# Two transformer blocks on one Trainium2 core: the expert layer's dense planes in two arithmetics, its stream buffers and its vector work rearranged

## The chip, the core and the metric

The kernel runs on one core of one Trainium2 chip. A core has five engines that follow their own instruction lists in order and wait for each other by semaphores: TensorE (PE in the profile; its weight loads have a row of their own, PEld), VectorE (DVE), ScalarE (ACT), GpSimd (POOL) and SyncE (SP), which here only starts transfers. Data are in SBUF (128 partitions); products accumulate in PSUM banks of 512 fp32 columns. The metric is the device time of one execution in microseconds (us), lower is better.

## The reference, cut to what matters

Two blocks follow each other on a sequence of 256 tokens of width 1024. The first has two kinds of attention and then the expert layer, the second has convolution, attention, retention, attention to a memory and a squared-relu MLP. The change is in the expert layer and in the few instructions on either side of it:

```python
def peer_ffn(x, w_query, sub_keys, expert_down, expert_up):
    ...
        q = (xc @ w_query).reshape(C, PEER_HEADS, 2, PEER_HALF)
        sc = jnp.einsum('thpd,hpnd->thpn', q, sub_keys).astype(jnp.float32)
        top_s, top_i = lax.top_k(sc, PEER_TOPK)
        ...
        best_s, best_pos = lax.top_k(cand_s, PEER_TOPK)
        experts = jnp.take_along_axis(cand_i, best_pos, axis=-1)
        gates = jax.nn.softmax(best_s, axis=-1)
        u = expert_down[experts]
        vv = expert_up[experts]
        act = jax.nn.gelu(jnp.einsum('cd,chkd->chk', xc, u).astype(jnp.float32), approximate=False)
        w = (gates * act).astype(xc.dtype)
        return jnp.einsum('chk,chkd->cd', w, vv)
```

There are 8 heads, 128 sub-keys on each of two sides, so 16384 experts, of which each token takes 16 per head: 128 experts per token.

## The kernel before, in words

The expert layer does not gather all its experts. For the last ND = 192 tokens it computes every expert: the 16384 rows of each table are cut into 128 planes of 128 experts, and a plane (512 KB, a tile of 128 x 1024 fp32) goes through TensorE whole. Only for the first NS = 64 tokens are rows gathered, by indirect transfers on POOL, 128 rows of 1024 numbers at a time.

**Queries.** `norm_d` makes the normed input in two parts, `xh` + `xl` (tiles `fh`, `fl`; type float32r, the sum is the fp32 value). 16 chunks of `peer_query` come by `stream`: SP loads `raw`, ACT rounds it to `hi` (line 61), DVE takes `lo` = raw - hi (line 62), and `gemm_t` makes three products per 128 rows: hi with xh, hi with xl, lo with xh (lines 98 to 100). `xf` (tile `ff`) = xh + xl for the 192 tokens is added on POOL. `rows` = the normed input of the first 64 tokens, scaled by a gain row that comes by DMA (line 647).

**Lists.** For each half t of the tokens DVE picks the top 16 scores and the best 16 pairs per head (lines 665 to 729). The result, `lists`, is transposed by TensorE (line 732) into `i1T`, `i2T`, `powT`, `gT`. The two halves share scratch, and a scheduler mixes their instructions on DVE.

**The first stage** runs over the 128 planes of the down table, two at a time. `stream_whole` loads a plane into any of nine buffers (three each of the tags raw, hi, lo), and `whole_plane` multiplies it in fp32 with `xf`, 8 products of 192 columns per plane (line 817); in the trace each of them is two MATMUL records and two LDWEIGHTS records. Into these planes three other things are woven: `gates_of` (from plane J0 = 34 on) builds one-hot tables for TG = 4 tokens on DVE and ACT (lines 797 to 802) and TensorE multiplies them into a gate table (line 806) that is written over, or multiplied into, `slots`; ACT applies gelu to each pair of planes; and `step` handles one gathered row per call: 64 times `dot` (line 751: fetched row times `rows`, summed), then 64 times `axpy` (line 761: fetched row times a scalar, added to `sums`). KD = 92 of the 128 steps are spread over the planes from plane 24 on, the other 36 over the first 112 planes of the second stage. `fetched` has five buffers.

**The second stage** runs over the 128 planes of the up table. Each comes by `stream` (three `raw`, three `hi`, three `lo` buffers); ACT and DVE make `a2` from `slots` (lines 879 to 881), and `ups` does ten products of 512 columns per plane (lines 865 to 870). The last LASTN = 3 planes are held back so that the sums of the two halves end one after the other. For the first 64 tokens the sum sits in other partitions than the residual: ACT copies it (`moved`, line 894), DVE adds twice. Norm and transposes of the next stage follow.

The order of instructions on each engine is set by the tile scheduler from the program; `tc.keep_in_program_order` pins an instruction to its place. `tc.high_priority` lets `split` go ahead of other work.

Of the kernel before, what the change touches and what calls it, by code (L numbers as in the profile page):

```python
# [40 lines left out]
def layers_kernel(ctx: ExitStack, tc: tile.TileContext, a: dict, out: bass.AP, upto: str = "all"):  # L41
# [28 lines left out]

    def stream(src):
        if ahead:
            return ahead.pop(0)
        raw = stream_p.tile([P, CH], F32, name="raw", tag="raw", bufs=3)
        nc.sync.dma_start(raw, src)
        own = more["at"] % (3 + more["n"]) < 3
        more["at"] += 1
        pool, b = (stream_p, 3) if own else (more["pool"], more["n"])
        hi = pool.tile([P, CH], F32R, name="hi", tag="hi", bufs=b)
        lo = pool.tile([P, CH], F32R, name="lo", tag="lo", bufs=b)  # L80
        with tc.high_priority():
            split(raw, hi, lo)
        return hi, lo
# [486 lines left out]
    with ExitStack() as c2:  # L570
# [3 lines left out]
        xl = fx.tile([P, KT, T], F32R, name="fl")  # L574
        xf = pr.tile([P, KT, ND], F32, name="ff")
        slots = pr.tile([P, P, ND], F32, name="slots")
        TG = 4
        NG = T // TG
# [24 lines left out]
        rs_peer = norm_d(x_sb, ss_peer, 1, xh, xl, prs)  # L603
        G.tensor_tensor(xf, f32v(xh[:, :, NS:]), f32v(xl[:, :, NS:]), op=OP.add)


        def fetched():
            return pr.tile([P, D], F32, name="fetched", tag="fetched", bufs=5)

# [14 lines left out]

        ranks = carve([P, 2, 16, P], BF)
        for hq in range(4):
            pss = [at_tile() for _ in range(NT)]
            for q in range(4):
                hp = hq * 4 + q
                o = mm_tile()  # L630
                gemm_t(o[:, :T], xh, xl, stream(a["peer_query"][hp]))
                qT = prs.tile([P, T], F32, name="qT", tag="oh1")
                S.copy(qT, o[:, :T])
                if hq > 0 and q < 3:
                    c = (hq - 1) * 3 + q
                    if c < 8:
                        rs, cs = ranks[:, c // 4, c % 4 * 4:c % 4 * 4 + 4], iota16b[:, c // 4, c % 4 * 4:c % 4 * 4 + 4, None]
                        tc.keep_in_program_order(S.copy(rs, cs.to_broadcast([P, 4, P])))
# [5 lines left out]
        grow = fetched()  # L644
        nc.scalar.dma_start(grow, bass.AP(tensor=a["ffn_gain"].tensor, offset=0, ap=[[0, P], [1, D]]))
        rows = pr.tile([P, D], F32, name="rows_s", tag="rows_s")
        V.scalar_tensor_tensor(rows[:NS], x_sb[:NS, 0, :], rs_peer[0][:NS], grow[:NS], op0=OP.mult, op1=OP.mult)
        S.copy(rows[NS:], rows[:NS])
        tc.keep_in_program_order(V.tensor_copy(iota, iota_f[:, :, None].to_broadcast([P, P, 2])))
# [5 lines left out]
        powT = pr.tile([P, T], BF, name="powT")  # L655
        gT = [pr.tile([P, T], dt, name="gT%d" % i) for i, dt in enumerate((F16, F32))]
        floor = top[0]
        for t in range(NT):
# [37 lines left out]
            for i in range(2):  # L696
                V.copy_predicated(keyu[:, i, :], keyu[:, 4, :], keyu[:, 2 + i, :])
            lists = carve([P, 5, P])
            oh = carve([P, 16, P], BF)
# [29 lines left out]
            V.tensor_tensor(scaled, scaled, inverse, op=OP.mult)  # L729
            tp = tp_tile()  # L730
            for i in range(4):
                PE.transpose(tp[:, i * P:(i + 1) * P], lists[:, i, :], ident)
            ts = slice(t * P, (t + 1) * P)
            S.copy(i1T[:, ts], tp[:, 0:P])
            S.copy(i2T[:, ts], tp[:, P:2 * P])
            S.copy(powT[:, ts], tp[:, 3 * P:4 * P])
            S.copy(gT[0][:, ts], tp[:, 2 * P:3 * P])
            V.tensor_tensor(gT[1][:, ts], tp[:, 2 * P:3 * P], gT[0][:, ts], op=OP.subtract)

# [13 lines left out]

        sums = pr.tile([P, D], F32, name="sums")

# [28 lines left out]
        def gates_of(g, j):  # L784
# [3 lines left out]

            shape = [P, TG // 2, P, 2]
            oh1, oh2 = (prs.tile(shape, dt, name=n, tag=n) for n, dt in (("oh1", BF), ("oh2", F16)))  # L790
            og = [prs.tile(shape, F16, name="og%d" % i, tag="og%d" % i) for i in range(2)]
            places = iota[:, None, :, :].to_broadcast(shape)
# [8 lines left out]
            for k in range(TG):  # L801
                S.mul(og[1][:, k // 2, :, k % 2], oh2[:, k // 2, :, k % 2], gT[1][:, g * TG + k:g * TG + k + 1])
            ps = at_tile()
            for k in range(TG):
                for i in range(2):
                    PE.matmul(ps[:, k * P:(k + 1) * P], oh1[:, k // 2, :, k % 2], og[i][:, k // 2, :, k % 2],
                              start=(i == 0), stop=(i == 1))
            gv = ps.rearrange("p (t j) -> p j t", t=TG)
            sv = slots[:, :, cs]
            if j > 0:  # L810
                V.tensor_tensor(sv[:, :j], gv[:, :j], sv[:, :j], op=OP.mult)
            if j < P:
                S.copy(sv[:, j:], gv[:, j:])

# [6 lines left out]
        K0 = 12  # L821
        KD = 92
        for jp in range(P // 2):
# [5 lines left out]
            while state["k"] < KD * (jp - K0 + 1) // (P // 2 - K0):  # L829
                step()  # L830
            nt = state["g"] * TG - NS
            o = mm_tile()
            for jj in range(2):
                whole_plane(o[:, jj * ND:(jj + 1) * ND], stream_whole(a["peer_down"][j + jj]))
            ov = o[:, :2 * ND].rearrange("p (j t) -> p j t", j=2)
# [37 lines left out]
        for j in range(P):  # L873
            while state["k"] < min(2 * HALF, KD + -(-(2 * HALF - KD) * (j + 1) // KU)):
                step()
            uh, ul = stream(a["peer_up"][j])

            a2 = prs.tile([P, 7 * NS], F32R, name="a2", tag="oh1")
            S.copy(a2[:, :ND], slots[:, j, :])  # L879
            S.copy(a2[:, ND:T], slots[:, j, :NS])  # L880
            V.tensor_tensor(a2[:, T:], slots[:, j, :], f32v(a2[:, :ND]), op=OP.subtract)
            if j >= P - LASTN:
                held.append((j, (uh, ul, a2)))
            else:
                for t in range(NT):
                    ups(j, (uh, ul, a2), t)
        moved = fetched()
# [472 lines left out]
```

## Time and profile before

| what | value |
|---|---|
| median of 3 runs | 1474.74 us (1473.08 to 1474.85) |
| the profiled execution | 1476.18 us, of which the span from the first to the last instruction is 1474.4 us |
| mean granted TensorE clock | 0.996 |
| TensorE busy | 1429.4 us, 97% of the span |
| VectorE, ScalarE, GpSimd busy | 982.8 us, 716.4 us, 265.5 us |
| moved from and to memory | 336.90 MB, 228 GB/s over the span |

A busy share is a mean over stages that have different limits. The expert layer takes about half of the span: queries from about 158 us, the first stage from 226 to 589 us, the second from 589 to 923 us. A TensorE record is drawn until its results are out, so that records overlap: the distance from one start to the next tells what an instruction costs in a full stream, not its drawn length.

### The profile page before, as it was taken

How to read it: one execution, taken by the hardware profiler on the slowest of the kernel's cores; microseconds unless marked ns; L12 is line 12 of the kernel's file. 1: busy time of each engine (PE TensorE's matmuls, PEld its weight loads, DVE VectorE, ACT ScalarE, POOL GpSimd, SP SyncE). 2: the span in 40 equal slices, each digit the busy share in tenths (PEclk: the TensorE clock that was granted, in tenths of full speed). 3: DMA queues.
4: the chain of work that ended last, by engine and by line, in shares of the span. 5: the costliest groups of instructions: out<-in, count | busy, mean ns of one | idle time of the engine just before them, and what ended most of it. 6: DMA issues, size and time to landing. Idle time of an engine off the chain costs nothing. (4 is left out here: it accounts for less than half of the span.)

```text
span 1474.4 us, 23648 instructions
## 1 busy us (share of the span) xinstructions
PE 1429.4 (97%) x8728; PEld 1265.8 (86%) x8728; DVE 982.8 (67%) x1884; ACT 716.4 (49%) x1448; POOL 265.5 (18%) x223
## 2 busy tenths in 40 slices
PE   9999899999999999989999999899999999999998
PEld 7778799999999999667676778797899989899886
DVE  7975568957767776767766776554475555566653
ACT  6565552224333332555555565574444455565442
POOL 4621100134343323211111100031101100000000
PEclk9999999999999999999999999999999999999999
DMA  7434558599999998878878767544356554366553
GB/s 271 153 125 158 177 188 298 193 382 349 341 351 337 351 347 301 295 251 267 263 252 274 260 213 228 198 156 140 118 169 192 186 186 155 125 205 192 192 186 115
DMA packets 93700, 336.90 MB, mean 228 GB/s; under 512 B 10736, under 2 KB 12656, under 8 KB 92816
## 3 DMA queue, kind: packets, MB, share of 16 engines
q1 hardware_dynamic: 73376, 259.79, 52.7%
q0 software_dynamic: 19344, 73.41, 14.0%
q10 hardware_dynamic: 864, 2.19, 0.4%
q8 instruction: 69, 1.13, 0.3%
q14 instruction: 47, 0.39, 0.1%
HBM read 331.15 MB, written 4.19 MB: 227 GB/s over the span
## 5 line engine op out<-in xcount | busy, mean ns | idle before, releaser
L62 DVE TENSOR_TENSOR lo<-raw,hi 128x1024 fp32r<-128x1024 f32 x356 | 439.4, 1235 | 303.6 <-ACT hi L61 302.5
L61 ACT CAST hi<-raw 128x1024 fp32r<-128x1024 f32 x356 | 373.3, 1049 | 413.8 <-PE mm L99 112.9
L817 PE MATMUL mm<-ff,whole 128*128 128x192 f32 x2048 | 345.3, 328 | 0.0
L817 PEld LDWEIGHTS mm<-ff,whole 128*128 128x128 f32 x2048 | 333.2, 191 | 0.0
L98 PE MATMUL mm<-rows_h,hi 128*128 128x256 f32 x736 | 204.0, 283 | 2.1 <-ACT qT_x L1198 1.1
L100 PE MATMUL mm<-rows_h,lo 128*128 128x256 f32 x736 | 204.6, 280 | 1.0 <-DVE lo L62 1.0
L99 PE MATMUL mm<-rows_l,hi 128*128 128x256 f32 x736 | 204.8, 280 | 0.0
L98 PEld LDWEIGHTS mm<-rows_h,hi 128*128 128x128 f32 x736 | 137.4, 189 | 3.6 <-ACT hi L61 1.4
L100 PEld LDWEIGHTS mm<-rows_h,lo 128*128 128x128 f32 x736 | 138.5, 189 | 1.6 <-DVE lo L62 1.6
L99 PEld LDWEIGHTS mm<-rows_l,hi 128*128 128x128 f32 x736 | 138.6, 189 | 0.6
L745 POOL DMA_INDIRECT fetched<-in_peer_up,picks x64 | 77.3, 1208 | 274.7 <-DVE sums L761 255.0
L838 ACT ACTIVATE slots<-mm 128x384 f32<-128x384 f32 (+43 forms) x60 | 22.4, 373 | 200.2 <-PE mm L817 200.1
L868 PE MATMUL mm<-hi,a 128*128 128x512 f32 x256 | 103.3, 403 | 16.6 <-ACT a L879 16.5
L745 POOL DMA_INDIRECT fetched<-in_down_rows,picks x64 | 81.5, 1273 | 176.9 <-DVE fetched L751 105.1
L865 PE MATMUL mm<-hi,a 128*128 128x512 f32 x256 | 104.2, 407 | 3.4 <-ACT a L879 2.4
L866 PE MATMUL mm<-lo,a 128*128 128x512 f32 x256 | 101.5, 396 | 0.0
L869 PE MATMUL mm<-lo,a 128*128 128x512 f32 x256 | 101.3, 396 | 0.0
L870 PE MATMUL mm<-hi,a 128*128 128x512 f32 x256 | 81.1, 397 | 0.0
L761 DVE SCALAR_TENSOR_TENSOR sums<-fetched,acts,sums 128x1024 f32<-128x1024 f32 x63 | 80.5, 1277 | 0.1
L751 DVE SCALAR_TENSOR_TENSOR fetched<-fetched,rows_s 128x1024 f32<-128x1024 f32 x64 | 75.8, 1216 | 6.3 <-DMA fetched<-in_down_rows,picks 6.3
L868 PEld LDWEIGHTS mm<-hi,a 128*128 128x128 f32 x256 | 48.1, 188 | 35.6 <-ACT a L879 24.7
L865 PEld LDWEIGHTS mm<-hi,a 128*128 128x128 f32 x256 | 48.2, 188 | 27.9 <-ACT a L879 8.1
(376 smaller groups left out, 2506.6 us busy)
## 6 DMA issues: line engine op xcount, KB each, us to landing
whole<-in_peer_down SPq DMA_DIRECT2D x128, 512.0 KB, 5.7
raw<-in_peer_up SPq DMA_DIRECT2D x128, 512.0 KB, 4.6
raw<-in_w_in_2t SPq DMA_DIRECT2D x52, 512.0 KB, 3.5
raw<-in_w_up SPq DMA_DIRECT2D x32, 512.0 KB, 4.3
raw<-in_w_down SPq DMA_DIRECT2D x32, 512.0 KB, 4.3
raw<-in_w_in SPq DMA_DIRECT2D x24, 512.0 KB, 3.9
raw<-in_peer_query SPq DMA_DIRECT2D x16, 512.0 KB, 4.1
raw<-in_w_in_2n SPq DMA_DIRECT2D x12, 512.0 KB, 3.4
```

What stands on the lines that cost most here:

```text
L61: S.copy(hi, src)
L62: V.tensor_tensor(lo, src, f32v(hi), op=OP.subtract)
L98: PE.matmul(o, hi, xh[:, k, :], start=(k == 0), stop=False)
L99: PE.matmul(o, hi, xl[:, k, :], start=False, stop=False)
L100: PE.matmul(o, lo, xh[:, k, :], start=False, stop=(k == kts - 1))
L745: G.indirect_dma_start(out=r, out_offset=None, in_=tables[table], in_offset=bass.IndirectOffsetOnAxis(ap=picks[:, k:k + 1], axis=0))
L817: PE.matmul(o, w[:, k * P:(k + 1) * P], xf[:, k, :], start=(k == 0), stop=(k == KT - 1))
L865: PE.matmul(acc[0][hf], both, uh[:, ds], start=first, stop=False)
L866: PE.matmul(acc[0][hf], both, ul[:, ds], start=False, stop=last)
L868: PE.matmul(acc[1][hf], high, uh[:, ds], start=first, stop=False)
L869: PE.matmul(acc[1][hf], high, ul[:, ds], start=False, stop=False)
L870: PE.matmul(acc[1][hf], low, uh[:, ds], start=False, stop=last)
```

## The change

Eight edits in the expert layer, and what follows from the first for the order on POOL:

1. In the first stage, from plane JS = 24 on, every odd plane goes through `stream` and `gemm_t` instead of `stream_whole` and `whole_plane`: 24 products of 192 columns in float32r (hi with xh, hi with xl, lo with xh) in place of 8 in fp32. That is 52 planes.
2. KD falls from 92 to 76: 16 steps move to the second stage, which then has 52.
3. In the second stage `raw` gets six chunks: the three buffers of before for planes 0 to 2 of every six, then `raw_o` (in the memory of the one-hot tables, two buffers) for planes 3 and 5 and `raw_f` (in the memory of `xf`) for plane 4. The two ACT copies into `a2` are pinned to program order and written ahead of `stream`.
4. One-hot tables are built for TG = 8 tokens per call, in 128 x 1024 instructions; the products of a call go to two PSUM tiles of four tokens.
5. The transposes of `lists` are written at planes 14 and 28 (`turn`) and pinned; each half has a `lists` table of its own.
6. `xf` is added on DVE, and it and `rows` are written between the query groups.
7. `fetched` has four buffers, and `sums` shares memory with `rows`.
8. The sums for the first 64 tokens are added straight from PSUM; the ACT copies `moved` go.
9. Since split planes read `fh` and `fl` until the end of the first stage, the two loads of the memory's normed rows into that place (`nh`, `nl`, 1 MB each, on POOL), which are issued at the start of the first stage in the kernel before, stand after the 16th gather of up rows in POOL's list, that is at the end of the first stage.

```diff
-    def stream(src):
+    def stream(src, raw=None):
         if ahead:
             return ahead.pop(0)
-        raw = stream_p.tile([P, CH], F32, name="raw", tag="raw", bufs=3)
+        if raw is None:
+            raw = stream_p.tile([P, CH], F32, name="raw", tag="raw", bufs=3)
         nc.sync.dma_start(raw, src)
...
-        TG = 4
+        TG = 8
...
-        G.tensor_tensor(xf, f32v(xh[:, :, NS:]), f32v(xl[:, :, NS:]), op=OP.add)
...
-            return pr.tile([P, D], F32, name="fetched", tag="fetched", bufs=5)
+            return pr.tile([P, D], F32, name="fetched", tag="fetched", bufs=4)
...
+        def unsplit():
+            tc.keep_in_program_order(V.tensor_tensor(xf, f32v(xh[:, :, NS:]), f32v(xl[:, :, NS:]), op=OP.add))
+
+        def scaled_rows():
+            tc.keep_in_program_order(V.scalar_tensor_tensor(rows[:NS], x_sb[:NS, 0, :], rs_peer[0][:NS], grow[:NS],
+                                                            op0=OP.mult, op1=OP.mult))
+            tc.keep_in_program_order(S.copy(rows[NS:], rows[:NS]))
+
         for hq in range(4):
+            if hq in (1, 2):
+                (unsplit if hq == 1 else scaled_rows)()
...
-        V.scalar_tensor_tensor(rows[:NS], x_sb[:NS, 0, :], rs_peer[0][:NS], grow[:NS], op0=OP.mult, op1=OP.mult)
-        S.copy(rows[NS:], rows[:NS])
...
-            tp = tp_tile()
-            for i in range(4):
-                PE.transpose(tp[:, i * P:(i + 1) * P], lists[:, i, :], ident)
...
+            def turn(t=t, lists=lists):
+                tp = tp_tile()
+                for i in range(4):
+                    tc.keep_in_program_order(PE.transpose(tp[:, i * P:(i + 1) * P], lists[:, i, :], ident))
...
-        sums = pr.tile([P, D], F32, name="sums")
+        sums = pr.tile([P, D], F32, name="sums", tag="rows_s")
...
-        KD = 92
+        KD = 76
+        JS = 24
...
+            if j in (14, 28):
+                turns[j // 14 - 1]()
...
             for jj in range(2):
-                whole_plane(o[:, jj * ND:(jj + 1) * ND], stream_whole(a["peer_down"][j + jj]))
+                ot, src = o[:, jj * ND:(jj + 1) * ND], a["peer_down"][j + jj]
+                if j >= JS and jj == 1:
+                    gemm_t(ot, xh[:, :, NS:], xl[:, :, NS:], stream(src))
+                else:
+                    whole_plane(ot, stream_whole(src))
...
-            uh, ul = stream(a["peer_up"][j])
 
             a2 = prs.tile([P, 7 * NS], F32R, name="a2", tag="oh1")
-            S.copy(a2[:, :ND], slots[:, j, :])
-            S.copy(a2[:, ND:T], slots[:, j, :NS])
+            tc.keep_in_program_order(S.copy(a2[:, :ND], slots[:, j, :]))
+            tc.keep_in_program_order(S.copy(a2[:, ND:T], slots[:, j, :NS]))
+            raw = None
+            if j % 6 > 2:
+
+                raw = pr.tile([P, KT * ND], F32, name="raw_f", tag="ff")[:, :CH] if j % 6 == 4 else                     prs.tile([P, CH], F32, name="raw_o", tag="ohs")
+            uh, ul = stream(a["peer_up"][j], raw)
...
                 if t == 0:
-                    S.copy(moved[NS:, ds], acc[0][hf][:NS])
-                    V.tensor_tensor(x_sb[NS:, 0, ds], acc[0][hf][NS:], x_sb[NS:, 0, ds], op=OP.add)
-                    V.tensor_tensor(x_sb[NS:, 0, ds], moved[NS:, ds], x_sb[NS:, 0, ds], op=OP.add)
+                    for part in (acc[0][hf][NS:], acc[0][hf][:NS]):
+                        tc.keep_in_program_order(V.tensor_tensor(x_sb[NS:, 0, ds], part, x_sb[NS:, 0, ds], op=OP.add))
```

DVE's list while the queries are computed, first before, then with the change (`fl` are the low parts of the normed input, eight in all):

```order
L198 SCALAR_TENSOR_TENSOR fl<-tp,gcols,fh 128x256 x5
L647 SCALAR_TENSOR_TENSOR rows_s<-x_sb,rrow,fetched 64x1024
L649 CAST iota<-slots 128x256
L198 SCALAR_TENSOR_TENSOR fl<-tp,gcols,fh 128x256 x3
L62 TENSOR_TENSOR lo<-raw,hi 128x1024 x5
```

```order
L199 SCALAR_TENSOR_TENSOR fl<-tp,gcols,fh 128x256 x8
L62 TENSOR_TENSOR lo<-raw,hi 128x1024
L631 TENSOR_TENSOR ff<-fh,fl 128x1536
L62 TENSOR_TENSOR lo<-raw,hi 128x1024 x4
L634 SCALAR_TENSOR_TENSOR rows_s<-x_sb,rrow,fetched 64x1024
```

The scaled rows moved behind all eight `fl` and five `lo`, and the sum for `xf` came onto DVE.

DVE's list where the second half's lists are finished (the last `slots<-slots 128x16x8` of a half, line 709 before and 720 now, is what TensorE's transposes of it wait for), first before, then with the change:

```order
L798 TENSOR_TENSOR oh_3257<-iota,i2T 128x512
L706 TENSOR_TENSOR slots<-slots 128x2048
L725 TENSOR_SCALAR slots<-slots 128x128
L708 TENSOR_TENSOR slots<-slots 128x1024
L726 TENSOR_SCALAR slots<-slots 128x128
L708 TENSOR_TENSOR slots<-slots 128x512
L728 TENSOR_SCALAR slots<-slots 128x128
L708 TENSOR_TENSOR slots<-slots 128x256
L729 TENSOR_TENSOR slots<-slots 128x128
L709 TENSOR_TENSOR slots<-slots 128x16x8
L738 TENSOR_TENSOR gT_2393<-tp,gT_2392 128x128
L751 SCALAR_TENSOR_TENSOR fetched,acts<-fetched,rows_s 128x1024 x8
```

```order
L766 SCALAR_TENSOR_TENSOR fetched,acts<-fetched,rows_s 128x1024 x3
L720 TENSOR_TENSOR slots<-slots 128x16x8
L62 TENSOR_TENSOR lo<-raw,hi 128x1024
L766 SCALAR_TENSOR_TENSOR fetched,acts<-fetched,rows_s 128x1024
L714 TENSOR_TENSOR slots<-slots 128x2048
L717 TENSOR_TENSOR slots<-slots 128x2048
L62 TENSOR_TENSOR lo<-raw,hi 128x1024
L766 SCALAR_TENSOR_TENSOR fetched,acts<-fetched,rows_s 128x1024 x2
L719 TENSOR_TENSOR slots<-slots 128x1024
L719 TENSOR_TENSOR slots<-slots 128x512
L719 TENSOR_TENSOR slots<-slots 128x256
L720 TENSOR_TENSOR slots<-slots 128x16x8
```

Six dots and two `lo` now stand ahead of the end of the lists in this piece, and one more dot and two more `lo` shortly above it; before, the first dot came after that end. On TensorE the first transpose of the first half stands at the same place in both kernels (after three products of plane 18). The last three of the second half stood after two products of plane 26 and now stand after ten products of plane 31.

## Rows read from the trace of the kernel before

**Rows 1.** Engines by stretch: busy us with count, clock, DMA share, GB/s

```profile
226.00:320.00 94.00, 91.77 (x561) 91.35 (x560) 77.68 (x382) 20.93 (x46) 16.98 (x15) 0.98 0.78 278
320.00:560.00 240.00, 240.00 (x1702) 237.22 (x1701) 177.94 (x400) 92.52 (x314) 88.60 (x74) 1.00 0.96 349
589.00:840.00 251.00, 231.97 (x945) 173.83 (x945) 176.12 (x220) 135.63 (x282) 44.46 (x33) 0.99 0.81 266
840.00:923.00 83.00, 82.06 (x348) 64.06 (x347) 58.12 (x74) 49.74 (x102) 0.00 (x0) 1.00 0.71 226
923.00:940.00 17.00, 13.02 (x59) 10.32 (x58) 13.73 (x21) 10.87 (x21) 3.22 (x4) 0.91 0.69 234
```

**Rows 2.** Timeline of TensorE, second stage: start, length, line, what

```profile
655.08 0.40 PE L868 MATMUL mm<-hi,a 128*128 128x512 f32 x1
...
657.41 0.40 PE L868 MATMUL mm<-hi,a 128*128 128x512 f32 x1
```

**Rows 3.** Waits in the second stage: us in total, times, longest

```profile
ACT hi L61 <- DMA raw<-in_peer_up: 61.3, 30, 3.7
...
PE mm L868 <- ACT a L879: 16.5, 14, 1.9
```

**Rows 4.** Timeline of ScalarE, second stage; idle time before it in brackets

```profile
660.38 1.04 ACT L61 CAST hi<-raw 128x1024 fp32r<-128x1024 f32 x1 [3.66 <-DMA raw<-in_peer_up]
```

**Rows 5.** Transfers of the up planes: count, KB each, median us to landing

```profile
raw<-in_peer_up SPq DMA_DIRECT2D x128, 512.0 KB, 4.6
```

**Rows 6.** Costliest groups of the page, VectorE: busy us, mean ns

```profile
L62 DVE TENSOR_TENSOR lo<-raw,hi 128x1024 fp32r<-128x1024 f32 x356 | 439.4, 1235 | 303.6 <-ACT hi L61 302.5
...
L761 DVE SCALAR_TENSOR_TENSOR sums<-fetched,acts,sums 128x1024 f32<-128x1024 f32 x63 | 80.5, 1277 | 0.1
```

**Rows 7.** Timeline of DVE, ACT and PE, queries

```profile
175.32 1.28 DVE L647 SCALAR_TENSOR_TENSOR rows_s<-x_sb,rrow,fetched 64x1024 f32<-64x1024 f32 x1 [4.91 <-DMA fetched<-in_ffn_gain]
...
177.25 0.39 PE L99 MATMUL mm<-fl,hi 128*128 128x256 f32 x1 [2.80 <-DVE fl L198]
```

**Rows 8.** Timeline of TensorE, first stage, fp32 planes between the transposes

```profile
276.68 0.33 PE L732 MATMUL tp<-ident,slots 128*128 128x128 f32 x1 [2.23 <-DVE slots L709]
276.84 9.97 PE L817 MATMUL mm<-ff,whole 128*128 128x192 f32 x50
...
299.44 0.49 PE L732 MATMUL tp<-ident,slots 128*128 128x128 f32 x3
299.77 20.32 PE L817 MATMUL mm<-ff,whole 128*128 128x192 f32 x124
```

**Rows 9.** DVE by line, first stage (320 to 560 us): busy us, mean ns

```profile
L751 DVE SCALAR_TENSOR_TENSOR fetched<-fetched,rows_s 128x1024 f32<-128x1024 f32 x56 | 66.3, 1216 | 0.0
...
L797 DVE TENSOR_TENSOR oh<-iota,i1T 128x512 bf16<-128x512 bf16 x46 | 19.2, 418 | 0.0
```

**Rows 10.** Timeline of TensorE, queries, 256 columns; 27 products from first to last

```profile
222.44 0.28 PE L98 MATMUL mm<-fh,hi 128*128 128x256 f32 x1
...
225.50 0.28 PE L100 MATMUL mm<-fh,lo 128*128 128x256 f32 x1
```

**Rows 11.** Timeline of TensorE, first block: fp32 products of 64 columns

```profile
131.42 1.89 PE L506 MATMUL mm<-vm,pT 128*128 128x64 f32 x16
133.15 1.04 PE L164 MATMUL tp<-ident,ho 128*128 128x128 f32 x8
```

**Rows 12.** Weight loads by shape, whole program: busy us, mean ns

```profile
L98 PEld LDWEIGHTS mm<-rows_h,hi 128*128 128x128 f32 x736 | 137.4, 189 | 3.6 <-ACT hi L61 1.4 <-ACT qT_x L1198 1.3 <-ACT rows_h L197 0.4
...
L806 PEld LDWEIGHTS <-oh 128*128 128x128 bf16 x384 | 25.8, 97 | 3.0
...
L506 PEld LDWEIGHTS mm<-vm,pT 128*128 128x128 f32 x48 | 5.9, 191 | 0.0
```

**Rows 13.** Timeline of TensorE behind the second stage

```profile
933.59 0.41 PE L190 MATMUL tp<-ident,xs 128*128 128x128 f32 x2 [1.68 <-issue]
936.30 1.12 PE L190 MATMUL tp<-ident,xs 128*128 128x128 f32 x6 [2.31 <-DVE xs L208]
```

More of the change, by code (lines that the diff above doesn't have):

```diff
@@ L574, in layers_kernel @@
         xl = fx.tile([P, KT, T], F32R, name="fl")
-        xf = pr.tile([P, KT, ND], F32, name="ff")
+        xf = pr.tile([P, KT, ND], F32, name="ff", tag="ff")
         slots = pr.tile([P, P, ND], F32, name="slots")
-        TG = 4
+        TG = 8
         NG = T // TG
@@ L625, in layers_kernel @@
         ranks = carve([P, 2, 16, P], BF)
+        grow = fetched()
+        nc.scalar.dma_start(grow, bass.AP(tensor=a["ffn_gain"].tensor, offset=0, ap=[[0, P], [1, D]]))
+        rows = pr.tile([P, D], F32, name="rows_s", tag="rows_s")
+        def unsplit():
[4 more added lines that the diff above has]
+            tc.keep_in_program_order(S.copy(rows[NS:], rows[:NS]))
         for hq in range(4):
+            if hq in (1, 2):
+                (unsplit if hq == 1 else scaled_rows)()
             pss = [at_tile() for _ in range(NT)]
@@ L642, in layers_kernel @@
                 S.copy(sc[t][:, hq * 4:hq * 4 + 4, :].rearrange("p a b -> p (a b)"), pss[t])
-        grow = fetched()
-        nc.scalar.dma_start(grow, bass.AP(tensor=a["ffn_gain"].tensor, offset=0, ap=[[0, P], [1, D]]))
-        rows = pr.tile([P, D], F32, name="rows_s", tag="rows_s")
-        V.scalar_tensor_tensor(rows[:NS], x_sb[:NS, 0, :], rs_peer[0][:NS], grow[:NS], op0=OP.mult, op1=OP.mult)
-        S.copy(rows[NS:], rows[:NS])
         tc.keep_in_program_order(V.tensor_copy(iota, iota_f[:, :, None].to_broadcast([P, P, 2])))
@@ L656, in layers_kernel @@
         gT = [pr.tile([P, T], dt, name="gT%d" % i) for i, dt in enumerate((F16, F32))]
+        turns = {}
+        tables_of = [carve([P, 5, P]) for _ in range(NT)]
         floor = top[0]
@@ L697, in layers_kernel @@
                 V.copy_predicated(keyu[:, i, :], keyu[:, 4, :], keyu[:, 2 + i, :])
-            lists = carve([P, 5, P])
+            lists = tables_of[t]
             oh = carve([P, 16, P], BF)
@@ L729, in layers_kernel @@
             V.tensor_tensor(scaled, scaled, inverse, op=OP.mult)
-            tp = tp_tile()
-            for i in range(4):
-                PE.transpose(tp[:, i * P:(i + 1) * P], lists[:, i, :], ident)
[L733 to L738, printed above, removed]
+            def turn(t=t, lists=lists):
+                tp = tp_tile()
+                for i in range(4):
+                    tc.keep_in_program_order(PE.transpose(tp[:, i * P:(i + 1) * P], lists[:, i, :], ident))
+                ts = slice(t * P, (t + 1) * P)
+                S.copy(i1T[:, ts], tp[:, 0:P])
+                S.copy(i2T[:, ts], tp[:, P:2 * P])
+                S.copy(powT[:, ts], tp[:, 3 * P:4 * P])
+                S.copy(gT[0][:, ts], tp[:, 2 * P:3 * P])
+                V.tensor_tensor(gT[1][:, ts], tp[:, 2 * P:3 * P], gT[0][:, ts], op=OP.subtract)
+            turns[t] = turn
         tables = {n: a[n].rearrange("a b d -> (a b) d") for n in ("down_rows", "peer_up")}
@@ L789, in gates_of @@
             shape = [P, TG // 2, P, 2]
-            oh1, oh2 = (prs.tile(shape, dt, name=n, tag=n) for n, dt in (("oh1", BF), ("oh2", F16)))
-            og = [prs.tile(shape, F16, name="og%d" % i, tag="og%d" % i) for i in range(2)]
+            oh1 = prs.tile(shape, BF, name="oh1", tag="oh1")
+            ohs = prs.tile([P, 2, TG // 2, P, 2], F16, name="ohs", tag="ohs")
+            oh2 = ohs[:, 0]
+            og = [ohs[:, 1], prs.tile(shape, F16, name="og1", tag="og1")]
             places = iota[:, None, :, :].to_broadcast(shape)
@@ L802, in gates_of @@
                 S.mul(og[1][:, k // 2, :, k % 2], oh2[:, k // 2, :, k % 2], gT[1][:, g * TG + k:g * TG + k + 1])
[L803 to L813, printed above, removed]
+            for part in range(0, TG, 4):
+                ps = at_tile()
+                for k in range(part, part + 4):
+                    c = (k - part) * P
+                    for i in range(2):
+                        PE.matmul(ps[:, c:c + P], oh1[:, k // 2, :, k % 2], og[i][:, k // 2, :, k % 2],
+                                  start=(i == 0), stop=(i == 1))
+                gv = ps.rearrange("p (t j) -> p j t", t=4)
+                sv = slots[:, :, cs.start + part:cs.start + part + 4]
+                if j > 0:
+                    V.tensor_tensor(sv[:, :j], gv[:, :j], sv[:, :j], op=OP.mult)
+                if j < P:
+                    S.copy(sv[:, j:], gv[:, j:])
         def whole_plane(o, w):
@@ L886, in layers_kernel @@
                     ups(j, (uh, ul, a2), t)
-        moved = fetched()
         for t in range(NT):
```

## The prediction

> **What bounds the kernel now.** I read the engines by stretch first [rows 1]. TensorE is drawn busy for all of 320 to 560 us, and for 232.0 of 251 us in the second stage as long as rows are gathered there. Where no row is gathered (840 to 923 us) it is busy for 82.1 of 83 us. So TensorE sets the pace of the first stage, and the second loses time beside the gathers.
>
> How much is lost is read from the distance of products. In the second stage the tenth product after the one at 655.08 us starts at 657.41 us: 0.233 us each, 2.33 us per plane [rows 2]. The 945 products of 589 to 840 us [rows 1] would need 220.2 us and took 251: 30.8 us lost. The 348 behind them would need 81.1 us and took 83: 1.9 us. Together 32.7 us over what TensorE needs.
>
> The waits say why [rows 3]. TensorE waits for ACT's `a2` (16.5 us in 14 waits; the rest hides in overlapping records). ACT's list has the rounding of the next plane ahead of this `a2`, and that rounding waits for the plane's transfer: 61.3 us in 30 waits, as at 660.38 us [rows 4]. Three `raw` chunks explain it: a chunk's place turns over every 3 x 2.33 = 7.0 us, of which rounding (1.04) [rows 4] and difference (1.24) [rows 6] take 2.3. That leaves 4.7 us for a transfer whose median landing is 4.6 us [rows 5]. Any delay by a gather is a stall.
>
> **Six raw chunks, the largest term.** A place then turns over every 14.0 us, and 14.0 - 2.3 = 11.7 us are left for a landing. The longest wait seen was 3.7 us [rows 3], so 7 us more cover every one. Two things can eat into this. The rate: 128 planes and 52 gathers, 52/112 of a chunk beside each of the first 112 planes, are 1.464 x 0.524 MB per 2.33 us = 329 GB/s; the first stage moves 349 GB/s while TensorE is busy throughout [rows 1], so it fits, closely. And `nh`, `nl`, 2.1 MB, now start with the second stage: 6 us of that rate. VectorE has room: 176.1 us busy over 94.5 planes [rows 1] is 1.86 us per plane, 16 more axpys of 1.277 us [rows 6] over 112 planes make it 2.04 of 2.33. The pinned `a2` copies change nothing by themselves: in ACT's list the next plane's rounding still precedes them. I let 5 of the 32.7 us stand: **-27.7 us** (bounds -33 and 0).
>
> **The scaled rows moved.** In the queries DVE stands at line 647 for 4.91 us for the gain row, three `fl` are queued behind it, and TensorE waits 2.80 us for one of them [rows 7]. Now all `fl` precede it: **-2.8 us**. The sum for `xf`, 128 x 1536, comes onto DVE behind them; the nearest row, 1.24 us for 128 x 1024 [rows 6], makes some 1.9 us of it. DVE has idle time there, and TensorE meets the queries' next `lo` with several chunks in hand, so I cost it at nothing; uncovered it is 1.9 us.
>
> **The transposes of the lists.** The first half's first transpose stays in plane 18, and DVE's work ahead of it stays too, so its stall of 2.23 us, and the 10 us after it in which 50 products take 9.97 us instead of 8.2 (the granted clock of this stretch is 0.98 [rows 1], part of it on the 1.2 GHz level), remain [rows 8]. The second half's change. Before, no wait is shown at 299.44 us, 22.8 us behind the first transpose [rows 8]. Now seven dots (1.216 us each [rows 9]) and four `lo` (1.235) are ahead on DVE, 13.4 us, and eight one-hot instructions of double length instead of ten short ones: between 8 and 16 times 0.418 us [rows 9], so up to 2.5 us more. The lists end 36 to 39 us behind the first transpose, later still if a dot waits for its gather. TensorE gets there after 13 planes of 2.6 us plus the 1.8 us of low clock: 36 us. A tie, at a place where a stall also costs clock: **+4 us** (bounds 0 and 9).
>
> **The split planes.** A whole plane is 16 records, 124 of which take 20.32 us: at most 0.164 us each, 2.62 us per plane [rows 8]. A split plane is 24 records of 192 columns in float32r, a shape that the trace does not have. Two rows bound it from below. Float32r products of 256 columns start 3.06/26 = 0.1177 us apart [rows 10], those of 512 columns 0.233 [rows 2]: 0.45 ns per column, which gives 0.0889 us for 192. But a product also loads 128 x 128 weights, and where columns are few the load shows: fp32 products of 64 columns start 1.73/16 = 0.108 us apart [rows 11]. The load record of float32r weights is as long as fp32's (189 against 191 ns; bf16 97) [rows 12]. So I take 0.108 us, the row that is like it in its load: 24 x 0.108 = 2.59 us, 0.03 less than whole. Over 52 planes **-1.6 us**. Bounds: 0.0889 gives -25; the 256-column distance gives 2.82 us per plane, +11; at the top, a product that costs what the fp32 product of 192 columns costs (two records, 0.328 us) gives +273.
>
> [...]
>
> VectorE must carry 52 `lo` more in the 294 us of planes 24 to 127: 64 us, less 16 dots, 19.5 us; one-hots between no change and 40 us less. From 177.9 of 240 us [rows 1], 218 of 294, it comes to 222 to 262 us, 89% at most. ACT takes 52 roundings, 55 us, on 39%. Both stay under TensorE. The look-ahead falls: nine buffers served one plane each, a split plane takes three, so nine hold 4.5 planes, some 11.8 us. That still covers the landing; see the rivals.
>
> **The end of the second stage.** TensorE waits 1.68 and 2.31 us for the norm [rows 13], at clock 0.91 [rows 1]. ACT's copies leave the chain and three `lo` move behind the norm in DVE's list: **-3 us** (bounds 0 and -5).
>
> **Hidden edits.** Eight-token tables issue the same products on TensorE. Four `fetched` buffers still give a gather over 15 us at one step per 3.9 us or more. `sums` in `rows`' place waits for the last dot, on the same engine.
>
> **The sum.** -27.7 - 2.8 + 4 - 1.6 - 3 = -31.1 us on the profiled execution's 1476.18 us: 1445.1. That execution is 1.4 us over the median of the runs, so **1444 us**, 2.1% faster. Its own range is 1434 to 1458. About 0.2%, 3 us, is what a measurement of this kernel can tell from no change.
>
> **Rivals.**
> *A. The float32r load does not bind.* The split product then costs 0.0889 us, a split plane 2.13 us, 25 us less in all. VectorE's up to 262 us would stand in 269, so I grant 22: **1422 us**. For it: the straight line through 256 and 512 columns. Against it: the equal load records [rows 12]. [...]
> *B. The shorter look-ahead starves the first stage.* If each of its 104 planes lost what a plane of the second loses beside gathers (30.8/94.5 = 0.33 us), that is +34: **1478 us**, about no change. Against it: 11.8 us of look-ahead against 7.0 in the second stage, and a lower rate than now.
> *C. The second stage's loss follows the gathers, not the chunks.* 30.8 us on 36 gathers is 0.86 us each; 52 of them lose 45 us instead of 31, and without the gain the time is 1444 + 27.7 + 14 = **1486 us**, slower. It decides from 0.65 us per gather on. For it: no loss where no row is gathered [rows 1]. Against it: the first stage carries more gathers per us with nine buffers and no wait, so depth is what differs.
> *D. A float32r product of 192 columns costs like fp32's.* **1718 us**; slower from 0.133 us per product on.
>
> **Chances.** Forecast 0.56, A 0.26, B 0.06 (half of it no change, half slower), C 0.08, D 0.04. So faster 0.82, the same 0.03, slower 0.15. The range leaves out C, D, half of B and the edges of A: 1414 to 1474 us.
>
> **What the profile would show.** Right: 24 products of a split plane within 2.6 us; ACT's wait for `raw` in the second stage nearly gone and its products at 0.233 us; no wait for `fl` in the queries; at most a few us at the second half's transposes. Wrong: split products 0.09 or 0.12 us apart; TensorE waiting for `lo` or `hi` in the first stage; DVE waiting for fetched rows with `lo` behind it; waits for `a2` or `hi` in the second stage as before.

## The result, and the profile after

The changed kernel takes 1458.53 us (median of 4 runs, 1456.47 to 1459.66) against 1474.8 us of the kernel before in the same comparison: ratio 0.9884, 95% interval 0.9859 to 0.9908, so 1.2% faster. The forecast was 1444 us, its whole range 1414 to 1474. The direction and the whole range held; the time is just above the forecast's own range (1434 to 1458), and the gain is about half of the one forecast (16.3 of 31 us).

The engines by stretch, columns as in [rows 1]:

```profile
320.00:560.00 240.00, 240.00 (x2019) 239.49 (x2018) 198.11 (x333) 132.03 (x346) 73.17 (x60) 1.00 0.88 310
589.00:840.00 251.00, 244.38 (x1053) 193.61 (x1052) 210.34 (x258) 150.40 (x311) 81.63 (x53) 0.99 0.94 333
```

TensorE is still drawn busy for all of 320 to 560 us. The second stage is now nearly full: 244.4 of 251 us, 1053 products where 945 ran before. The wait of [rows 3], 61.3 us in 30 waits of this stage and 67.0 in 32 of the whole program, is down to this (whole program: us in total, times, longest):

```profile
ACT hi L61 <- DMA raw<-in_peer_up: 7.0, 3, 3.6
```

But TensorE waits at other places. These are its largest waits, same columns; the first has no counterpart in the kernel before, where the others were 2.3 (and 1.7 in a second piece), 1.8 and 2.2 us:

```profile
PE mm L891 <- DVE a L911: 6.6, 1, 6.6
PE tp L191 <- DVE xs L209: 4.1, 1, 4.1
PE mm L101 <- DVE lo L62: 3.3, 3, 2.3
PE tp L745 <- DVE slots L720: 2.9, 2, 2.2
```

To see what each stage gave or took, I use marks that both traces have on TensorE: the first product of the first stage, the first product of the second, a pair at its end (line 870, now 896) that I call its last, and a wait for a rounding in the next attention. Timeline of TensorE, first before, then after:

```profile
226.06 3.42 PE L817 MATMUL mm<-ff,whole 128*128 128x192 f32 x20
...
588.70 0.53 PE L865 MATMUL mm<-hi,a 128*128 128x512 f32 x1
...
922.88 0.63 PE L870 MATMUL mm<-hi,a 128*128 128x512 f32 x2
...
949.81 0.38 PE L98 MATMUL mm<-rows_h,hi 128*128 128x256 f32 x1 [0.71 <-ACT hi L61]
```

```profile
222.26 3.42 PE L836 MATMUL mm<-ff,whole 128*128 128x192 f32 x20
...
589.23 0.39 PE L99 MATMUL mm<-fh,hi 128*128 128x192 f32 x1
589.45 0.27 PE L100 MATMUL mm<-fl,hi 128*128 128x192 f32 x1
...
591.91 0.27 PE L101 MATMUL mm<-fh,lo 128*128 128x192 f32 x1
598.80 0.76 PE L891 MATMUL mm<-hi,a 128*128 128x512 f32 x1 [6.62 <-DVE a L911]
...
603.20 0.49 PE L894 MATMUL mm<-hi,a 128*128 128x512 f32 x1
...
903.28 0.63 PE L896 MATMUL mm<-hi,a 128*128 128x512 f32 x2
...
932.47 0.39 PE L99 MATMUL mm<-rows_h,hi 128*128 128x256 f32 x1 [0.72 <-ACT hi L61]
```

The last split plane starts at 589.23 us and is through at 592.02, one product distance (0.11 us) behind its last start. The first ten products of the second stage take 4.40 us (598.80 to 603.20) where ten took 2.33 in [rows 2]: after the stall they run on the 1.2 GHz level for the most part. The granted clock of two stretches there, as a share of 2.4 GHz, is the number ahead of the last two:

```profile
595.00:600.00 5.00, 1.20 (x3) 1.04 (x4) 4.50 (x6) 1.66 (x6) 3.07 (x4) 0.66 1.04 416
600.00:605.00 5.00, 5.00 (x16) 3.93 (x16) 0.60 (x2) 1.45 (x3) 0.97 (x1) 0.66 1.06 420
```

So the account is:

| part | forecast | measured | how |
|---|---|---|---|
| queries (`fl` ahead of the rows) | -2.8 | -3.8 | 226.06 to 222.26 |
| first stage, list transposes and split planes | +4 - 1.6 | +7.2 | 362.6 to 369.8 (222.26 to 592.02) |
| stall between the stages | 0 | +6.8 | 592.02 to 598.80 |
| low clock behind it | 0 | +2.1 | 4.40 - 2.33 |
| second stage without that | -27.7 | -31.8 | 334.2 to 304.5, less 2.1 |
| end of the second stage | -3 | +2.3 | 26.9 to 29.2, to the last mark |
| sum | -31.1 | -17.2 | span 1474.4 to 1457.2 |

The forecast gain is there, and a little more; 9 us are lost at the hand-over between the stages, 7 in the split planes, and 5 against the forecast at the end. I had costed the first at nothing and the other two at a gain. Gains beyond the forecast, 5 us in the queries and the second stage, hide part of these losses. The size of the gain is known to some 5 us only: in the trace of e9, whose second stage is that of the kernel before, this stage takes 329.5 us and not 334.2.

**The hand-over.** Timeline of ScalarE, VectorE and SyncE there, in the changed kernel:

```profile
591.03 1.05 ACT L61 CAST hi<-raw 128x1024 fp32r<-128x1024 f32 x1 [3.62 <-DMA raw<-in_peer_up]
594.42 1.05 ACT L61 CAST hi<-raw 128x1024 fp32r<-128x1024 f32 x1 [2.33 <-DMA raw<-in_peer_up]
595.37 0.47 ACT L866 ACTIVATE mm<-mm 128x384 f32<-128x384 f32 x1
595.78 0.33 ACT L904 CAST a<-slots 128x192 fp32r<-128x192 f32 x1
```

```profile
595.50 1.23 DVE L62 TENSOR_TENSOR lo<-raw,hi 128x1024 fp32r<-128x1024 f32 x1 [0.96 <-ACT hi L61]
596.64 0.55 DVE L867 TENSOR_TENSOR slots<-mm,slots 128x384 f32<-128x384 f32 x1
597.11 1.28 DVE L776 SCALAR_TENSOR_TENSOR sums<-fetched,acts,sums 128x1024 f32<-128x1024 f32 x1
598.30 0.62 DVE L911 TENSOR_TENSOR a<-slots,a 128x192 fp32r<-128x192 f32 x2
```

```profile
578.80 9.76 SPq L76 DMA_DIRECT2D raw<-in_peer_up  x3
```

The copy into `a2` for up plane 0 needs nothing that is late: e1 below makes it 26 us earlier. It starts at 595.78 us because ACT's list has the roundings of up planes 1 and 2 and the gelu of the last pair ahead of it. The rounding of plane 2 waits until 594.42 for its transfer, the third of three loads that SyncE issued one after the other over 9.8 us, as the chunks came free. Then `lo`, gelu product and one axpy stand ahead of L911 on VectorE, and TensorE starts at 598.80. In ACT's list of the kernel before, the copies for planes 0 and 1 stand between the gelus of earlier pairs, 20 us ahead of the second stage:

```profile
569.02 0.61 ACT L879 CAST a<-slots 128x192 fp32r<-128x192 f32 x2
```

### The profile page after: what moved, and what is told of

The parts are those of the page before. It is cut to its first block, busy times and chain, and to the rows that moved or that the text cites. A ratio compares the mean times of both kernels' runs of the same rounds, so it can differ in the third digit from the quotient of the medians.

```text
span 1457.2 us, 24511 instructions
## 1 busy us (share of the span) xinstructions
PE 1424.1 (98%) x9144; PEld 1274.8 (87%) x9144; DVE 1032.0 (71%) x1841; ACT 769.4 (53%) x1497; POOL 282.9 (19%) x222
## 5 line engine op out<-in xcount | busy, mean ns | idle before, releaser
L836 PE MATMUL mm<-ff,whole 128*128 128x192 f32 x1216 | 209.1, 328 | 0.0
L836 PEld LDWEIGHTS mm<-ff,whole 128*128 128x128 f32 x1216 | 196.3, 190 | 0.0
L99 PE MATMUL mm<-fh,hi 128*128 128x192 f32 (+1 forms) x544 | 155.4, 289 | 0.7 <-ACT hi L61 0.5
L101 PE MATMUL mm<-fh,lo 128*128 128x192 f32 (+1 forms) x544 | 150.2, 277 | 2.3 <-DVE lo L62 2.3
L100 PE MATMUL mm<-fl,hi 128*128 128x192 f32 (+1 forms) x544 | 151.1, 279 | 0.0
L760 POOL DMA_INDIRECT fetched<-in_down_rows,picks x64 | 82.6, 1290 | 287.8 <-DVE fetched L766 152.0
L760 POOL DMA_INDIRECT fetched<-in_peer_up,picks x64 | 98.0, 1531 | 202.0 <-DVE sums L776 183.9
L891 PE MATMUL mm<-hi,a 128*128 128x512 f32 x256 | 101.8, 398 | 6.6 <-DVE a L911 6.6
L101 PEld LDWEIGHTS mm<-fh,lo 128*128 128x128 f32 x544 | 104.6, 192 | 2.5 <-DVE lo L62 2.5
L99 PEld LDWEIGHTS mm<-fh,hi 128*128 128x128 f32 x544 | 103.9, 192 | 1.1 <-ACT hi L61 1.0
L100 PEld LDWEIGHTS mm<-fl,hi 128*128 128x128 f32 x544 | 104.6, 192 | 0.1
L894 PE MATMUL mm<-hi,a 128*128 128x512 f32 x256 | 101.7, 397 | 0.7 <-ACT a L904 0.7
```

The lines of the kernel that those rows point to most:

```text
L99: PE.matmul(o, hi, xh[:, k, :], start=(k == 0), stop=False)
L100: PE.matmul(o, hi, xl[:, k, :], start=False, stop=False)
L101: PE.matmul(o, lo, xh[:, k, :], start=False, stop=(k == kts - 1))
L760: G.indirect_dma_start(out=r, out_offset=None, in_=tables[table], in_offset=bass.IndirectOffsetOnAxis(ap=picks[:, k:k + 1], axis=0))
L836: PE.matmul(o, w[:, k * P:(k + 1) * P], xf[:, k, :], start=(k == 0), stop=(k == KT - 1))
L891: PE.matmul(acc[0][hf], both, uh[:, ds], start=first, stop=False)
```

## The experiments

Each run stands beside runs of the kernel before on the same chip. Those had medians of 1476.4 (e1 to e4), 1477.7 (e5 to e8) and 1475.6 us (e9 to e11), so distances to the kernel before are compared, not times, and a range of times that was expected shifts by 1.6 to 2.9 us. The changed kernel's distance is -16.3 us.

**e1, the pins.** The two copies into `a2` are no longer pinned; the rest of the changed kernel is kept.

```diff
-            tc.keep_in_program_order(S.copy(a2[:, :ND], slots[:, j, :]))
-            tc.keep_in_program_order(S.copy(a2[:, ND:T], slots[:, j, :NS]))
+            S.copy(a2[:, :ND], slots[:, j, :])
+            S.copy(a2[:, ND:T], slots[:, j, :NS])
```

> The changed kernel, but with the two copies into a2 left to the scheduler as in the kernel before; in ACT's list those for up planes 0 and 1 then stand five planes earlier, ahead of the roundings of the up planes. Theory (the pinned copies stand behind the rounding of up plane 2 and the last gelu, and that rounding waits for its chunk): TensorE's stall of 6.6 us at the start of the second stage goes, and the slow products behind it, 8 to 9 us in all: 1449 to 1451 us. Rival (the up planes' transfers are late as such, since memory is busy at 0.9 to 1.05 there): TensorE then waits for hi or lo instead, and the time stays at 1457 to 1459.

Measured: 1452.75 us, 23.7 under before, ratio 0.9836 (0.982 to 0.9853): 7.4 us better than the changed kernel. The time is 1.8 us over the range expected, and the kernel before is 1.6 us slower here too. Timeline of ACT and of TensorE:

```profile
569.95 0.61 ACT L904 CAST a<-slots 128x192 fp32r<-128x192 f32 x2
...
585.27 1.06 ACT L61 CAST hi<-raw 128x1024 fp32r<-128x1024 f32 x1 [0.50 <-DMA raw<-in_peer_up]
589.41 1.05 ACT L61 CAST hi<-raw 128x1024 fp32r<-128x1024 f32 x1 [1.61 <-DMA raw<-in_peer_up]
```

```profile
592.30 0.27 PE L101 MATMUL mm<-fh,lo 128*128 128x192 f32 x1
592.41 0.42 PE L891 MATMUL mm<-hi,a 128*128 128x512 f32 x1
```

The copies are done 22 us before they are needed, and the first product of the second stage follows the last split plane at its normal distance, at full clock. Roundings of up planes wait for their transfers here too, by 0.50 and 1.61 us, but only TensorE's later planes need them: late transfers alone do not make the stall.

**e2, the last three pairs whole.**

```diff
-                if j >= JS and jj == 1:
+                if JS <= j < 122 and jj == 1:
```

> The changed kernel with the last three pairs of down planes whole, so 49 split planes. The split planes that hold raw, hi and lo chunks until the end are gone there, and in ACT's list only one rounding of an up plane stands ahead of the copies into a2. Theory (chunks held by split planes, and the pinned copies behind three roundings): the stall goes as well, 1449 to 1451 us. Rival (busy memory): 1457 to 1459. If the pins alone are the cause and the chunks play no part, ACT's list still has the pins, and only the number of roundings ahead of them changes: part of the stall stays, 1452 to 1456.

Measured: 1455.17 us, 21.2 under before, 0.9854 (0.9837 to 0.987). The stall is 3.2 us instead of 6.6: the third of the outcomes, part of it stays. The one rounding ahead of the copies is long done here; they stand behind the gelu of the last pair, which waits for that pair's products. Timeline of ACT:

```profile
590.81 0.47 ACT L866 ACTIVATE mm<-mm 128x384 f32<-128x384 f32 x1 [4.72 <-PE mm L836]
591.20 0.34 ACT L904 CAST a<-slots 128x192 fp32r<-128x192 f32 x1
```

**e3, no split plane** (`JS = 128`).

> The changed kernel without any split plane. My account of the trace: split planes cost 2.7 us on TensorE, one of them waits 2.3 us for its lo behind the lists on VectorE and brings 1 to 2 us of low clock, and the boundary to the second stage costs 8.8 us; all of it goes: 1442 to 1446 us. If the split planes pay for themselves (their gain hidden by the stalls): 1450 or more.

Measured: 1449.31 us, 27.1 under before, 0.982 (0.9803 to 0.9838). That is 3 us above the range that I expected, and the trace shows a stall that I had not expected. Timeline of TensorE and of ACT:

```profile
589.23 0.77 PE L891 MATMUL mm<-hi,a 128*128 128x512 f32 x1 [4.42 <-DVE a L911]
```

```profile
584.85 1.04 ACT L61 CAST hi<-raw 128x1024 fp32r<-128x1024 f32 x1 [4.72 <-PE mm L836]
585.80 0.47 ACT L866 ACTIVATE mm<-mm 128x384 f32<-128x384 f32 x1
586.21 0.33 ACT L904 CAST a<-slots 128x192 fp32r<-128x192 f32 x1
```

A stall of 4.4 us stands here too, without any split plane and without a wait for a transfer: the rounding ahead of the pinned copies waits for the last whole plane to leave its chunk, and the gelu for its products. So the pins cost 4.4 us and 1.5 of low clock (ten products take 3.82 us) by themselves: about 3.2 for a gelu ahead of the copies, as in e2, and 1 for a rounding. In the changed kernel that rounding also waits for a late transfer, which brings the rest. The first stage is 362.6 us (222.21 to 584.81), the same as before: the 7.2 us come with the split planes.

**e4, three raw chunks** (`if j % 6 > 2` becomes `if False`).

> The changed kernel with three raw chunks in the second stage instead of six. Theory (the chunks hold back the transfers, and 52 gathers make it worse than 36): the second stage loses some 31 to 45 us again, 1487 to 1502 us. Rival (the gain of the second stage came from elsewhere, the pinned copies or their place ahead of the stream): 1456 to 1465.

Measured: 1495.4 us (2 runs), 19.0 over before, 1.0124 (1.0104 to 1.0144). The old wait is back, and larger than the 67.0 us of before (whole program); 52 rows are gathered beside this stage now, not 36:

```profile
ACT hi L61 <- DMA raw<-in_peer_up: 85.8, 46, 5.1
```

From its first to its last product the second stage takes 342.1 us against 304.5 with six chunks.

**e5, the end as before** (ScalarE copies, VectorE adds twice, and these additions are not pinned).

```diff
+        moved = fetched()
...
-                    for part in (acc[0][hf][NS:], acc[0][hf][:NS]):
-                        tc.keep_in_program_order(V.tensor_tensor(x_sb[NS:, 0, ds], part, x_sb[NS:, 0, ds], op=OP.add))
+                    S.copy(moved[NS:, ds], acc[0][hf][:NS])
+                    V.tensor_tensor(x_sb[NS:, 0, ds], acc[0][hf][NS:], x_sb[NS:, 0, ds], op=OP.add)
+                    V.tensor_tensor(x_sb[NS:, 0, ds], moved[NS:, ds], x_sb[NS:, 0, ds], op=OP.add)
```

> The changed kernel with the sums of the first 64 tokens taken as before (ScalarE copies them, VectorE adds twice, nothing pinned). From the last product ahead of the norm to the last wait for a weight rounding behind it, the changed kernel takes 20.6 us and the kernel before 18.3. Theory (the pinned additions interleave badly on VectorE with the lo of the next weights, and the last norm waits for them): 2 to 3 us faster than the changed kernel, 18 to 20 us under the kernel before. Rival (the end was slower because the stage ends at another point of the next weights' transfers): no difference, 15 to 17.5 us under before.

Measured: 1458.04 us, 19.6 under before, 0.9864 (0.9836 to 0.9891). The intervals of this and of the changed kernel overlap, so the runs alone don't tell the two apart. In the traces, from the last product of the second stage (904.38) to the mark in the attention (931.25) it is 26.9 us, as before, against 29.2. Over all traces this stretch takes 28.7 to 30.1 us in the six kernels with the new end and 26.7 to 28.6 in the seven with the old one.

**e6, split planes from plane 34** (`JS = 34`, 47 of them).

> The changed kernel with the split planes from plane 34 on instead of 24, 47 instead of 52. Theory (five split planes need their lo while VectorE works off the lists; one waits 2.3 us and TensorE's clock falls): the first stage loses 3 to 4 us less, 19 to 20.5 us under the kernel before. Rival (a split plane costs the same wherever it stands, 7.2 us over 52): 0.7 us less, 16 to 17.5 us under before.

Measured: 1453.07 us, 24.6 under before, 0.9837 (0.9819 to 0.9854). More than expected. The first stage takes 366.4 us without the stall, 3.4 less than with 52 split planes, as expected; but the stall is 4.3 us instead of 6.6, which I had not expected. As in e3, the rounding ahead of the copies waits only for TensorE to leave its chunk. The last split planes are the same as in the changed kernel, and yet the first up planes' loads went out 4 us earlier (from 574.95 us): that the last split planes hold chunks does not by itself make the transfer late, and what does was not tried. Together the two parts are 5.7 us, and the spans of the two traces are 5.9 apart; the rest of the larger distance comes from the kernel before, which is 2.9 us slower on this chip. The cost of the five planes sits in VectorE's work on the lists. Timeline of TensorE in the changed kernel:

```profile
299.20 0.35 PE L101 MATMUL mm<-fh,lo 128*128 128x192 f32 x1 [2.34 <-DVE lo L62]
```

The `lo` of a split plane stands behind list instructions there, and behind the wait the granted clock is 0.50 from 300 to 303 us; in e6 no wait for `lo` stands in this stretch.

**e7 and e11, the best parts**: no split planes, unpinned copies, the end as before; the rest of the change stays.

> No split planes, the two copies into a2 unpinned, and the sums of the first 64 tokens as before; the rest as in the changed kernel. If the three losses add up (7 us of split planes and their waits, 4.4 plus 2 us of the boundary without split planes, 2 to 3 us at the end): 33 to 38 us under the kernel before, 1439 to 1443. If the boundary's wait comes back as a wait for another engine: 29 to 32 under.

Measured: 1443.08 us, 34.6 under before, 0.9771 (0.9751 to 0.9791).

> The kernel of e7 again, beside e10 on the same chip: 33 to 36 us under the kernel before.

Measured: 1443.43 us, 32.2 under before, 0.9777 (0.9756 to 0.9798). That is a little less than expected, and it beats both kernels. The two runs are 18.3 and 15.9 us better than the changed kernel; the three losses of the account are 7, 6 to 9 and 2 us, so they add up within the noise. In e7's second stage (columns as above) next to nothing is left to gain:

```profile
589.00:840.00 251.00, 249.89 (x1068) 196.42 (x1067) 215.97 (x266) 154.92 (x321) 79.39 (x48) 1.00 0.93 330
```

**e8, the split planes alone**, put into the kernel before.

> The kernel before with the split planes from 24 on and nothing else. My account: TensorE's first stage gets 2.7 us longer by its products, 3 to 5 us by lo that stands behind the lists on VectorE, and the boundary costs nothing since the copies into a2 are not pinned: 5 to 10 us slower than before. Rival (a split plane is faster and the losses come from the other edits): the same as before or faster. Rival (with 92 gathers in the first stage VectorE is then the bound): 15 us slower or more.

Measured: 1486.7 us, 9.0 over before, 1.0072 (1.0051 to 1.0093). The first stage takes 371.3 us against 362.6, and the second stage follows the first with no stall: the copies are not pinned there. As expected.

**e9, the scaled rows alone**, moved between the query groups of the kernel before and pinned.

> The kernel before with one edit: the scaled rows are written between the query groups and pinned, so that all eight fl and five lo stand ahead of them on VectorE. Theory (the 2.8 us wait for fl was exposed): 2.8 to 4 us faster than before. Rival (the queries' chunks arrive late anyway, and the wait turns up at the next rounding): no difference.

Measured: 1470.11 us, 5.5 under before, 0.997 (0.995 to 0.9991). The first stage starts at 222.41 us, 3.65 earlier than in the trace of before, as the theory has it; the interval reaches from 1 to 7 us, so the runs don't narrow the size down further. The trace's span is 8.0 us shorter, but the other 4.65 us lie in the second stage, which this edit leaves as it was.

**e10, later transposes**: e7 with `turn` at planes 20 and 32.

> As e7, with the transposes of the two halves written at planes 20 and 32, so that TensorE meets them 13 and 27 products later. Theory (the 2.2, 0.4 and 1.7 us that TensorE waits there are exposed, and the low clock follows from them): 4 to 7 us faster than e7, 1436 to 1440 us. Rival (the one-hot tables and gates behind them become late instead): no faster than e7, or slower.

Measured: 1443.57 us, 32.1 under before, beside 1443.43 of e11: no difference. The wait moved. TensorE no longer waits at the first transpose, but at the next three of the same half, for a later instruction of the lists:

```profile
282.93 0.73 PE L745 MATMUL tp<-ident,slots 128*128 128x128 f32 x3 [2.82 <-DVE slots L737]
```

My expectation fell; as this trace has it, VectorE's list work, not the place of the transposes, sets this time.

## Why the prediction was only half right

**Six raw chunks (-27.7, measured -31.8): right.** Between its marks the second stage has 1290 distances of 0.2333 us, 301.0 us, and takes 304.5, 2.1 of which is low clock. e4 shows that the chunks do it. Rival C's mechanism shows with three chunks only. There the stage takes 342.1 us with 52 gathers against 334.2 with 36, or 329.5 in e9's trace; less 2 of low clock, 16 more gathers cost 6 to 11 us, 0.4 to 0.7 each and not 0.86, if they are all that differs. With six chunks they cost nothing that shows.

**The pinned copies: this step failed.** The prediction said that they "change nothing by themselves: in ACT's list the next plane's rounding still precedes them". That is so in the middle of the stage, where I had read it. At its start the kernel before has the copies for planes 0 and 1 among the gelus of the last down planes, 20 us ahead of the stage's first product, and the pins take that away. e1 and e3 show the cost: 4.4 to 6.6 us of stall and 1.5 to 2 of clock. The sentence on the split planes' look-ahead, "That still covers the landing", held inside the first stage (rival B did not come) but not at the hand-over, where a rounding waits 2.3 us for its transfer.

**The split planes (-1.6, measured +7.2): the size was off, and a wait was missing.** A split plane's products start (591.91 - 589.45)/22 = 0.112 us apart, not 0.108. 47 of them with the planes between and behind take 271.7 us in e6 (316.69 to 588.37) and 267.9 in e3 (316.91 to 584.81): 0.08 us more than a whole plane each, 4.2 us for 52. The other 3 us come from the wait of 2.34 us for a `lo` behind the lists, one of the signs of being wrong that I had named, and some 1.6 us of low clock behind it, less 1 us that TensorE waits less at the transposes than in e3; I had put the lists into the transposes' term alone. Rival A is out: a product of 192 columns costs 0.112 and not 0.0889 us. The row that I took the 0.108 us from was misread: the 16 records of [rows 11] are eight fp32 products, two records each, so 0.108 us is the distance of records and an fp32 product of 64 columns costs 0.216. A record has one weight load, so the comparison of loads stands; that it came within 4% is not proof of it. The Trainium skill, TensorE: Matmul & The Clock Gate, section Back-to-back issue gap, gives N/2.4 + 2.5 ns for an isolated product, by which 82.5 ns is the estimate for 192 columns, and says that this counts too little at few columns in a stream that loads weights for every product. The 112 ns of this trace agree with that.

**The transposes (+4, measured 0).** In e3 TensorE waits 4.3 us at them, 2.1 more than before, in the direction forecast; yet the stage is not longer. The traces show what gives the 2 us back: the low clock behind the first wait, which I had said would remain. Granted clock (the number ahead of the last two) behind the same wait of 2.2 us, before and in e3, and the records behind it (two make a product) in e3 and e11:

```profile
276.00:280.00 4.00, 3.32 (x15) 3.32 (x16) 4.00 (x22) 0.00 (x0) 0.00 (x0) 0.75 0.03 12
```

```profile
273.00:277.00 4.00, 4.00 (x26) 4.00 (x26) 4.00 (x24) 0.00 (x0) 0.00 (x0) 1.00 0.28 74
```

```profile
273.00 8.94 PE L836 MATMUL mm<-ff,whole 128*128 128x192 f32 x54
```

```profile
272.99 10.62 PE L836 MATMUL mm<-ff,whole 128*128 128x192 f32 x54
```

The clock stays up in the traces of the changed kernel, e1 to e5 and e7 (8.94 us for these 54 records) and falls in those of before, e6, e8, e9 and e11. Since e7 and e11 are the same kernel, this differs from one execution to the next; that the term came out at 0 is luck.

**The scaled rows (-2.8): right**, measured 3.8 in the changed kernel and 3.65 in e9; the row of the wait showed most of it.

**The end (-3, measured +2.3): wrong in sign.** I counted ACT's copies as leaving the chain and did not follow what then stands where. Timeline of ScalarE and of TensorE in the changed kernel:

```profile
913.01 1.04 ACT L61 CAST hi<-raw 128x1024 fp32r<-128x1024 f32 x1 [1.86 <-DMA raw<-in_w_in_2t]
913.96 0.62 ACT L172 ACTIVATE junk<-x_sb 128x512 bf16<-128x512 f32 x1
```

```profile
916.59 0.87 PE L191 MATMUL tp<-ident,xs 128*128 128x128 f32 x6 [4.06 <-DVE xs L209]
```

The squares of the last half (L172) stand behind a rounding of the next weights that waits for its transfer, and TensorE waits 4.06 us in one piece instead of 1.68 and 2.31 [rows 13]. Together these are as long. So the step of taking the copies off the chain gained nothing: from the last product to the first of the attention it is 14.5 us before, 14.7 in the changed kernel and 14.5 in e5. The loss comes behind that product: 12.4 us to the mark before, 12.3 in e5, 14.5 in the changed kernel. First products and granted clock, before and then after:

```profile
937.41 1.01 PE L98 MATMUL mm<-rows_h,hi 128*128 128x256 f32 x3
940.00:942.00 2.00, 2.00 (x18) 2.00 (x18) 0.48 (x1) 0.64 (x2) 0.00 (x0) 0.95 1.01 413
```

```profile
917.96 1.01 PE L99 MATMUL mm<-rows_h,hi 128*128 128x256 f32 x3 [0.49 <-ACT rows_h L198]
922.00:924.00 2.00, 2.00 (x11) 2.00 (x10) 0.48 (x1) 0.61 (x2) 0.00 (x0) 0.50 0.42 172
```

The 1.2 GHz level lasts some 6 us behind the first product instead of 3, and 0.68 us go to a wait for `rows_l`. e5 shows that the edit as a whole costs this; that the wait in one piece is what keeps the clock down longer is read from the traces alone.

## What to carry to other kernels

Pinning an instruction cost nothing that shows where it stood anyway and much where the scheduler had moved it: read the order at the first and last turns of the loop, not only in its middle. Deepening the buffers that a stage's transfers wait for paid in full; at the hand-over from the stage before, check what stands ahead of the first product on every engine. When an edit moves a wait, look for the next instruction of the same list behind it: later transposes only waited for a later instruction of the lists.

## What the runs showed of the hardware that I had not expected

Float32r products of 192 columns start 0.112 us apart and those of 256 columns 0.1177 [rows 10]: a quarter fewer columns save 5%. The fp32 records of 64 columns, two of which make a product, start 0.108 us apart [rows 11], hardly less. Where columns are this few, the distance hardly falls with them; that the weight load is the reason fits the equal load records [rows 12], but no run here changed the load alone.

The granted clock can fall or stay up behind the same wait of the same kernel: 54 records behind a wait of 2.2 us take 8.94 us in e7 and 10.62 in e11. What decides it, no run here shows.
